# Forgetting attention with plain fp32 values and turned probabilities, the value product of a head pair in two column groups, and sums of squares added up before one reduction

## The chip, the core and the metric

The kernel runs on one core of a Trainium2 chip. The metric is the device time of one execution in microseconds, median of the runs shown. Five engines work side by side, each through its own queue of instructions in a fixed order: PE (matrix products and transposes through the array; its weight loads are listed apart as PEld), DVE (vector work), ACT (activations, copies with a scale), POOL (vector work in SBUF, and issuing of DMAs) and SP (issuing of DMAs). Data lies in SBUF (128 partitions) and in PSUM, where matrix products come out.

## What is computed

One layer for 1024 tokens of width 1024, in fp32, of three sub-layers with RMS norms and residual adds: token mixing, cross-attention to 256 memory tokens, and a SwiGLU feed-forward part. The change lies in token mixing, whose parts are these:

```python
h = rms_norm(x, mix_pre_g); proj = h @ w_in            # u | q | k | v | f_logit
y_ssm = s5_mixer(u, ...)                               # ends in the GLU below
y_fox = forgetting_attention(q, k, v, f_logit)         # 8 heads of 64
y_mix = concat([rms_norm(y_ssm, ssm_out_g), rms_norm(y_fox, fox_out_g)])
x = x + rms_norm(y_mix @ w_out, mix_post_g)
...
g = gelu(y); out = g * sigmoid(g @ glu_w + glu_b)      # end of s5_mixer
...
s = (q @ k.T) * scale + cum_log_f[i] - cum_log_f[j]    # causal, per head
p = softmax(s); out = p @ v                            # per head
```

Both branches are normalised over their 512 channels, so for each token the sum of squares over all channels of `y_ssm`, and over all heads of `y_fox`, is needed.

## The kernel before, in words

**Precision.** Most products are made of three fp32r matmuls (`mm3`, lines 121 to 124): each operand is split (`split`, lines 112 to 119) into a high part, rounded to fp32r by an ACT copy, and the rest, subtracted by DVE; high x high, high x low and low x high are added up in PSUM. Some products are plain fp32 matmuls without splits, which stand in the trace as two instructions each; among them are the sums over partitions with a column of ones (line 237) and the SSM products at lines 485, 537 and 649 to 650. Line 537 puts its 32 weight columns into one of four column groups of the array (`tile_position`).

**Stages.** The input projections and the SSM scan come first, then an attention stage, in which GLU, the SSM half of the output product and the memory tiles run as fillers, then the attention half of the output product, cross-attention and the feed-forward part. The attention stage is driven by `paced(fox(yf), (gp, 0, RATE))` (lines 903 and 1018): after every step of the attention generator about one step of the fillers is traced (`fillers`, line 979: the last v tiles, GLU, `mem_load`, 16 memory tiles, the rest of the output rows, `build_a(0)`). A scheduler then puts each engine's instructions in an order by their place in the program, by priorities and by when their operands and buffers are expected to be free; on the chip that order is fixed.

**v.** `v_tiles` (line 297) makes v in two column halves c of 256 columns (four heads), eight token tiles each. A tile leaves PSUM by an ACT copy with the row scale, is split into high and low (line 300), the two lying side by side per head, and goes to DRAM tensor `v_d` by POOL's queue (line 325). `load_v` (line 805) brings back a head pair by SP's queue.

**Attention** (`fox`, line 705). The loop at line 818 runs over 8 heads x 8 query tiles t of 128 tokens. `scores` is two steps ahead: matmuls, bias and minimum on DVE, exponent on ACT, scaling by the reciprocal sum on DVE or POOL. `turn` (line 761) transposes the probabilities on PE, up to four blocks of 128 to a PSUM bank, and takes them out by `split` (line 772: ACT copy, then DVE subtraction) into two slabs per head and pair of query tiles. `values` (line 774) runs one step later, for each head after every odd t, over a column block of 256 tokens, qc = t // 2: for each of its 2 qc + 2 key tiles two matmuls (lines 782 and 783), whose weights are v's high and low parts together (128 columns), with the high and then the low probabilities moving. So the two halves of PSUM's partitions hold two sums, which ACT (line 789) and DVE (line 790) add; the result is split with its gain (line 791) into `yf`, and squared by ACT.

**Sums of squares.** For heads 0 and 1, each column block's squares are summed over partitions at once by `token_sums` (line 233: two matmuls with ones, and a small DVE copy or addition). From head 2 on, they are added up in a tile `total`, on POOL from head 4 on (line 803), and summed over partitions once at the end (line 840). In `glu` (line 665), each of 8 blocks of 512 tokens x 128 channels is squared by ACT (line 691) and goes through `token_sums` with four matmuls (line 690).

**Buffers.** Large tiles come from a pool of 16 slabs of 8 KB per partition (line 59). The smaller tags of line 193 have one to three buffers; "d" has one, and holds GLU's squares first, `total` later.

`mem_load` (line 955) multiplies the memory tokens by their row scales, four 256-column tiles in one DVE instruction (line 962), ahead of their splits.

## Time and profile before

| | us |
|---|---|
| median of 3 runs | 1432.68 |
| lowest to highest | 1431.65 to 1433.4 |
| span of the profiled execution | 1428.8 |

The profiled execution is told by its span, the time from its first to its last instruction; the runs' times also hold what lies around it. The largest groups of its instructions by busy time are the matmuls of the feed-forward part:

```profile
L1277 PE MATMUL x<-slab,op 128*128 128x512 f32 x984 | 233.3, 389 | 0.5 <-DVE op L115 0.5
L1277 PE MATMUL g<-slab,op 128*128 128x512 f32 x744 | 178.7, 389 | 0.0
```

A row of this view names the line, the engine, the operation, what it writes and reads, its shape and type and how often it ran; then its busy time in us, the mean duration of one in ns, and the idle time of the engine just before, with what ended it. The duration of a matmul includes its way through the array: the next one starts earlier, so the distance of two starts is what a matmul holds PE for. In a timeline, the columns are the start in us from the span's start, the busy time in us, engine, line, operation and how many instructions are merged; an idle time of the engine follows in brackets with its releaser. In a table of stretches, each engine's busy time is followed by its number of instructions, and PEclk is the granted share of PE's clock. In a list of waits, the numbers are the total in us, how often, and the longest.

### The profile page before, as it was taken

The page shows a single profiled execution, that of the slowest core. Times are in us where ns is not written, and L with a number is a line of the kernel's source. Part 1 is how long each engine was busy: PE and PEld are TensorE (multiplying, and loading weights), DVE is VectorE, ACT ScalarE, POOL GpSimd, SP SyncE. Part 2 cuts the span into 40 slices and gives each one's busy share as a digit, 9 for nine tenths or more (in the row PEclk, how much of TensorE's full clock was granted, in tenths as well). Part 3 has the DMA queues.
Part 4 walks back from the last instruction along what each step waited for, and adds up shares of the span by engine and source line. Part 5 has one row for each costly group of instructions (what it writes and reads, how often), then busy time and mean ns, then how long its engine had stood idle before and what let it go on. Part 6 is the DMA issues. An engine that isn't in the chain of part 4 may idle for free.

```text
span 1428.8 us, 20846 instructions
## 1 busy us (share of the span) xinstructions
PE 1390.7 (97%) x7422; PEld 1187.5 (83%) x7422; DVE 1003.7 (70%) x1818; ACT 708.0 (50%) x1421; POOL 410.9 (29%) x432
## 2 busy tenths in 40 slices
PE   7999999999999898999999999999999999999997
PEld 6889898889989886788888788888888888888886
DVE  7839947877888876645557677887766676565565
ACT  6373347777888754543434533333333334444341
POOL 0001000022243134001111367676666661000021
PEclk9999999999999999999999999999999999999999
DMA  6325654165654658323637455454444446965444
GB/s 204 98 80 148 183 192 132 33 204 178 193 153 120 172 164 276 134 74 109 193 112 236 149 190 173 168 181 154 164 156 162 162 155 227 334 219 192 177 162 162
DMA packets 112824, 238.43 MB, mean 167 GB/s; under 512 B 11848, under 2 KB 48712, under 8 KB 112592
## 3 DMA queue, kind: packets, MB, share of 16 engines
q1 hardware_dynamic: 96576, 182.01, 39.8%
q0 software_dynamic: 16144, 55.09, 10.6%
q8 instruction: 58, 0.95, 0.3%
q14 instruction: 46, 0.38, 0.1%
HBM read 168.90 MB, written 76.81 MB: 172 GB/s over the span
## 4 chain that ended last, share of the span: by engine, by line
PE 58%; DVE 1%; DMA 1%; ACT 0%; issue 0%; DVEq 0%; SPq 0%; ACTq 0%
PE x L1277 17%; PE g L1277 13%; PE x L1535 7%; PE g L1535 7%; PE x L123 2%; PE x L124 2%; PE x L122 2%; PE g L122 2%; PE g L124 2%; PE g L123 2%; PE g L1065 1%; DMA a<-t_d 1%; PE g L1173 1%; DVE slab L115 0%; DVE whl L115 0%; DVE c L1056 0%
## 5 line engine op out<-in xcount | busy, mean ns | idle before, releaser
L1277 PE MATMUL x<-slab,op 128*128 128x512 f32 x984 | 233.3, 389 | 0.5 <-DVE op L115 0.5
L1277 PEld LDWEIGHTS x<-slab,op 128*128 128x128 f32 x984 | 184.6, 188 | 39.3 <-DVE op L115 1.0
L1277 PE MATMUL g<-slab,op 128*128 128x512 f32 x744 | 178.7, 389 | 0.0
L115 DVE TENSOR_TENSOR slab<-slab 128x1024 fp32r<-128x1024 f32 (+2 forms) x92 | 110.2, 1207 | 84.7 <-ACT slab L113 82.8
L1277 PEld LDWEIGHTS g<-slab,op 128*128 128x128 f32 x744 | 139.6, 188 | 29.0
L122 PE MATMUL g<-slab,whl 128*128 128x512 f32 (+1 forms) x416 | 151.7, 365 | 0.6 <-ACT whl L113 0.4
L123 PE MATMUL g<-slab,whl 128*128 128x512 f32 (+1 forms) x416 | 148.4, 357 | 0.0
L124 PE MATMUL g<-slab,whl 128*128 128x512 f32 (+1 forms) x416 | 148.2, 357 | 0.0
L113 ACT ACTIVATE slab<-slab 128x1024 fp32r<-128x1024 f32 (+2 forms) x92 | 94.8, 1037 | 106.4 <-DMA slab<-hs_d 81.5
L1535 PE MATMUL g<-slab 128*128 128x512 f32 x462 | 126.6, 389 | 0.0
L1535 PE MATMUL x<-slab 128*128 128x512 f32 x462 | 126.6, 389 | 0.0
L1535 PEld LDWEIGHTS g<-slab 128*128 128x128 f32 x462 | 86.7, 188 | 18.0
L1535 PEld LDWEIGHTS x<-slab 128*128 128x128 f32 x462 | 86.7, 188 | 18.0
L122 PE MATMUL g<-whl,slab 128*128 128x256 f32 (+2 forms) x288 | 87.5, 309 | 9.6 <-ACT whl L113 7.3
L115 DVE TENSOR_TENSOR op<-slab,op 128x512 fp32r<-128x512 f32 x80 | 83.9, 1059 | 11.6 <-ACT op L113 11.3
L1353 POOL TENSOR_TENSOR wt<-wt 128x256 f32<-128x256 f32 x88 | 84.2, 957 | 19.9 <-DMA wt<-in_w_down 16.3
L113 ACT ACTIVATE op<-slab 128x512 fp32r<-128x512 f32 x80 | 50.0, 627 | 77.7 <-PE x L1277 37.5
L122 PEld LDWEIGHTS g<-slab,whl 128*128 128x128 f32 x416 | 78.6, 189 | 11.8 <-ACT whl L113 0.6
L124 PEld LDWEIGHTS g<-slab,whl 128*128 128x128 f32 x416 | 78.4, 189 | 11.6 <-DVE whl L115 0.2
L115 DVE TENSOR_TENSOR whl<-raw,whl 128x1024 fp32r<-128x1024 f32 (+2 forms) x61 | 72.0, 1184 | 22.3 <-ACT whl L113 21.7
L123 PEld LDWEIGHTS g<-slab,whl 128*128 128x128 f32 x416 | 78.6, 189 | 10.6
L123 PE MATMUL g<-whl,slab 128*128 128x256 f32 (+2 forms) x288 | 86.1, 299 | 0.0
(394 smaller groups left out, 3149.3 us busy)
## 6 DMA issues: line engine op xcount, KB each, us to landing
hs_d<-ev POOLq DMA_DIRECT2D x77, 256.0 KB, 2.6
slab<-hs_d SPq DMA_DIRECT2D x35, 512.0 KB
wt<-in_w_down SPq DMA_DIRECT2D x44, 256.0 KB
wt_d<-wt POOLq DMA_DIRECT2D x22, 512.0 KB, 4.8
slab<-in_w_gate SPq DMA_DIRECT2D x20, 512.0 KB
slab<-in_w_up SPq DMA_DIRECT2D x20, 512.0 KB
slab<-wt_d SPq DMA_DIRECT2D x20, 512.0 KB
wd_d<-in_w_down SPq DMA_DIRECT2D x33, 256.0 KB
```

Source lines behind the costliest of these rows:

```text
L113: first = act.activation(out=hi, in_=src, func=AF.Copy, scale=1.0 if mul is None else mul)
L115: (lo_eng or dve).tensor_tensor(out=lo, in0=src, in1=hi.bitcast(F32), op=ALU.subtract)
L122: pe.matmul(ps, lh, rh, start=first, stop=False)
L123: pe.matmul(ps, lh, rl, start=False, stop=False)
L124: pe.matmul(ps, ll, rh, start=False, stop=last)
L1065: pe.transpose(tp[:, k], src[:, (k0 + k) * P:(k0 + k + 1) * P], ident)
L1173: turned = pe.transpose(tp[:, k], h3[:, (4 * n + k) * P:(4 * n + k + 1) * P], ident)
L1277: pe.matmul(ps, x[:, k], y[:, k], start=first and k + n == 0, stop=k == 3 and n == 2, skip_group_check=not first)
L1353: pool.tensor_tensor(out=o, in0=x, in1=y, op=ALU.subtract)
L1535: pe.matmul(banks[n][j], xo[:, u, js], wo[:, v], start=ends[0] and k == 0, stop=ends[1] and k == 2, skip_group_check=onto is not None)
```

## The change

- v stays in fp32: `v_tiles` writes the scaled copy as it is, `v_d` and its loads have half the size, and a load holds two head pairs (`load_v(0)` and `load_v(1)`).
- `turn` takes the turned probabilities out in fp32 by one copy, by DVE and ACT in turn. Three slabs hold a head's (column blocks 0 and 2 share one), until the odd head of the pair is done.
- `values` runs per head pair, after the odd head: for each key tile one fp32 matmul per head, with 64 weight columns each, head 0 in array columns 0 to 63 and head 1 in 64 to 127. The two heads' results then stand in the 128 partitions of one PSUM tile, and go straight from there into the split and the square.
- Squares of all head pairs are added up in `total`, and GLU's rows in `acc`; each is summed over partitions once.
- `mem_load` multiplies tile by tile.

```diff
--- before.py
+++ after.py
@@ -176,7 +176,7 @@
         return rb
 
     qk_d = dram.tile([8, P, S], F32, name="qk_d")
-    v_d = dram.tile([NT, P, 2 * 512], F32, name="v_d")
+    v_d = dram.tile([NT, P, 512], F32, name="v_d")
     h_d = dram.tile([16, NG, HP + P], F32, name="h_d")
     T_d = dram.tile([2, P, 16 * P], F32, name="T_d")
     nc_d = dram.tile([NH, S], F32, name="nc_d")
@@ -230,15 +230,12 @@
         rsqrt_mean(r, ps, D)
         return r, row_bcast(r, L)
 
-    def token_sums(sv, sq, first, p0=0, p1=P):
+    def token_sums(sv, sq):
         n = sv.shape[1]
         ps = g_ps([P, n])
         for j in range(n):
-            pe.matmul(ps[:, j:j + 1], sq[:, j * P:(j + 1) * P], ones[p0:p1, 0:1], start=True, stop=True)
-        if first:
-            dve.tensor_copy(sv, ps)
-        else:
-            dve.tensor_tensor(out=sv, in0=ps, in1=sv, op=ALU.add)
+            pe.matmul(ps[:, j:j + 1], sq[:, j * P:(j + 1) * P], ones[:, 0:1], start=True, stop=True)
+        dve.tensor_copy(sv, ps)
 
     def proj_tile(w, xH, xL, evac, ahead=False):
         halves = []
@@ -295,9 +292,6 @@
         stA.dma_start(out=qk_d[i], in_=o)
 
     def v_tiles(c, xH, xL, r):
-        def evac(ps, r, j, vf, vo):
-            act.activation(out=vf, in_=ps, func=AF.Copy, scale=r[:, j:j + 1])
-            split(vo[:, :, 0], vo[:, :, 1], vf.rearrange("p (h d) -> p h d", d=64))
         if c == 0:
             ws = load_vf()
             ftok = tt("yt", [P, NT, NH])
@@ -312,17 +306,11 @@
                 wh, wl = ws[k // 4]
                 mm3(ps, xH[k][:, ts], xL[k][:, ts], wh[:, k % 4], wl[:, k % 4], k == 0, k == KT - 1)
             vf = t2t([P, 256])
-            if c == 0:
-                vo = t2t([P, 4, 2, 64], F32R)
-            else:
-                if j % 2 == 0:
-                    pair = tt("a", [P, 2, 4, 2, 64], F32R)
-                vo = pair[:, j % 2]
             with tc.high_priority(offset=boost):
-                evac(ps[:, 0:256], r, j, vf, vo)
+                act.activation(out=vf, in_=ps[:, 0:256], func=AF.Copy, scale=r[:, j:j + 1])
                 if c == 0:
                     act.activation(out=ftok[:, j], in_=ps[:, 256:n], func=AF.Copy, scale=r[:, j:j + 1])
-            stA.dma_start(out=v_d.rearrange("t (c j) d -> j (t c) d", j=L)[j, :, c * 512:c * 512 + 512], in_=vo.rearrange("p h t d -> p (h t d)").bitcast(F32))
+            stA.dma_start(out=v_d.rearrange("t (c j) d -> j (t c) d", j=L)[j, :, c * 256:c * 256 + 256], in_=vf)
             yield
 
     def load_vf():
@@ -671,7 +659,7 @@
             split(hl[:, 0], hl[:, 1], w)
             gw.append(hl)
         sv = const.tile([P, NT], F32, name="sv_s")
-        sq, sums = tt("d"), []
+        acc = tt("d")
         for ct in range(4):
             cs = slice(ct * P, (ct + 1) * P)
             hl = slab([P, 2, S])
@@ -686,14 +674,15 @@
                 dve.tensor_tensor(out=y, in0=gl[ct][:, 0, hs].bitcast(F32), in1=gl[ct][:, 1, hs].bitcast(F32), op=ALU.add)
                 dve.scalar_tensor_tensor(out=y, in0=th, scalar=1.0, in1=y, op0=ALU.add, op1=ALU.mult)
                 split(hl[:, 0, hs], hl[:, 1, hs], y, g_out[:, ct:ct + 1])
-                while sums:
-                    token_sums(*sums.pop())
-                act.activation(out=sq[:, hs], in_=y, func=AF.Square)
-                sums.append((sv[:, 4 * h:4 * h + 4], sq[:, hs], ct == 0))
+                if ct == 0:
+                    act.activation(out=acc[:, hs], in_=y, func=AF.Square)
+                else:
+                    act.activation(out=th, in_=y, func=AF.Square)
+                    dve.tensor_tensor(out=acc[:, hs], in0=acc[:, hs], in1=th, op=ALU.add)
                 if h == 1:
                     ys.append(hl)
                 yield
-        token_sums(*sums.pop())
+        token_sums(sv, acc)
         ys_stat.append(sv)
 
     def glu_stats():
@@ -759,62 +748,60 @@
             units[h, t] = sc
 
         def turn(h, t):
-            tt = t % 2
-            if tt == 0:
-                pts[h, t // 2] = slab([P, 8, 256]), slab([P, 8, 256])
-            pth, ptl = pts[h, t // 2]
+            odd = t % 2
+            if t in (0, 2, 6):
+                p = slab([P, 8, 256], F32)
+                if t == 0:
+                    pts[h, 0], pts[h, 2] = p[:, 0:2], p[:, 2:8]
+                else:
+                    pts[h, t // 2] = p
+            pt = pts[h, t // 2]
             sc = units.pop((h, t))
             for k0 in range(0, t + 1, 4):
                 n = min(4, t + 1 - k0)
                 tp = g_ps([P, 4, P])
                 for k in range(n):
                     pe.transpose(tp[:, k], sc[:, (k0 + k) * P:(k0 + k + 1) * P], ident)
-                split(pth[:, k0:k0 + n, tt * P:(tt + 1) * P], ptl[:, k0:k0 + n, tt * P:(tt + 1) * P], tp[:, :n])
-
-        def values(h, qc):
-            r0 = (h % 2) * 64
-            pth, ptl = pts[h, qc]
+                o = pt[:, k0:k0 + n, odd * P:(odd + 1) * P]
+                if (t + k0 // 4) % 2:
+                    dve.tensor_copy(o, tp[:, :n])
+                else:
+                    act.activation(out=o, in_=tp[:, :n], func=AF.Copy)
+
+        def values(hp, qc):
             yp = g_ps([P, 256])
             nk = 2 * qc + 2
             for k in range(nk):
-                w = vs[h // 2][:, k, h % 2]
                 c0 = P if k == nk - 1 else 0
-                pe.matmul(yp[:, c0:], w, pth[:, k, c0:], start=k == 0, stop=False)
-                pe.matmul(yp[:, c0:], w, ptl[:, k, c0:], start=False, stop=k == nk - 1)
-            ft, qs_ = h // 2, slice(qc * 256, qc * 256 + 256)
-            if h % 2 == 0 and qc == 0:
+                for hh in range(2):
+                    w = vs[hp // 2][:, k, (hp % 2) * P + hh * 64:(hp % 2) * P + hh * 64 + 64]
+                    pe.matmul(yp[hh * 64:hh * 64 + 64, c0:], w, pts[2 * hp + hh, qc][:, k, c0:],
+                              start=k == 0, stop=k == nk - 1, tile_position=(0, 64 * hh))
+            qs_ = slice(qc * 256, qc * 256 + 256)
+            if qc == 0:
                 yf.append(slab([P, 2, S]))
-            w = tt("yt", [P, 256])
-            y, sq = w[r0:r0 + 64], w[64 - r0:P - r0]
-            act.activation(out=w[0:64], in_=yp[64:P], func=AF.Copy)
-            dve.tensor_tensor(out=y, in0=yp[0:64], in1=w[0:64], op=ALU.add)
-            split(yf[ft][r0:r0 + 64, 0, qs_], yf[ft][r0:r0 + 64, 1, qs_], y, g_out[r0:r0 + 64, 4 + ft:5 + ft])
-            if h < HA:
-                act.activation(out=sq, in_=y, func=AF.Square)
-                later.append((sv[:, 2 * qc:2 * qc + 2], sq, h == 0, 64 - r0, P - r0))
-                return
-            if h == HA and qc == 0:
-                sums.append(tt("d"))
-            total = sums[0][64 - r0:P - r0, qs_]
-            if h < HA + 2:
-                act.activation(out=total, in_=y, func=AF.Square)
+                if hp == 0:
+                    totals.append(tt("d"))
+            total, = totals
+            split(yf[hp][:, 0, qs_], yf[hp][:, 1, qs_], yp, g_out[:, 4 + hp:5 + hp])
+            if hp == 0:
+                act.activation(out=total[:, qs_], in_=yp, func=AF.Square)
             else:
-                act.activation(out=sq, in_=y, func=AF.Square)
-                pool.tensor_tensor(out=total, in0=total, in1=sq, op=ALU.add)
-
-        def load_v(hp):
-            v = slab([P, NT, 2, P])
-            sp.dma_start(out=v.rearrange("p j h d -> p j (h d)").bitcast(F32),
-                         in_=v_d[:, :, hp * 256:hp * 256 + 256].rearrange("j p c -> p j c"))
-            vs[hp] = v
+                sq = tt("yt", [P, 256])
+                act.activation(out=sq, in_=yp, func=AF.Square)
+                pool.tensor_tensor(out=total[:, qs_], in0=total[:, qs_], in1=sq, op=ALU.add)
+
+        def load_v(c):
+            v = slab([P, NT, 256], F32)
+            sp.dma_start(out=v, in_=v_d[:, :, c * 256:c * 256 + 256].rearrange("j p c -> p j c"))
+            vs[c] = v
 
         seq = [(h, t) for h in range(NH) for t in range(NT)]
-        HA, sums = 2, []
+        totals = []
         lag = 2
         vs = {}
         drain(prepare(0))
         load_v(0)
-        later = []
         for n in range(-lag, len(seq) + 1):
             if n + lag < len(seq):
                 h, t = seq[n + lag]
@@ -823,21 +810,17 @@
                     nxt = prepare(h + 1)
                 if t % 2 and h + 1 < NH:
                     step(nxt)
-                if t == 5 and h % 2 and h + 1 < NH:
-                    load_v(h // 2 + 1)
+                if (h, t) == (3, 5):
+                    load_v(1)
             if 0 <= n < len(seq):
                 h, t = seq[n]
                 turn(h, t)
             yield
             if 0 < n:
                 h, t = seq[n - 1]
-                if t % 2:
-                    values(h, t // 2)
-                    if len(later) > 1 or h >= HA and later:
-                        token_sums(*later.pop(0))
-        while later:
-            token_sums(*later.pop(0))
-        token_sums(sv, sums[0], False)
+                if t % 2 and h % 2:
+                    values(h // 2, t // 2)
+        token_sums(sv, totals[0])
         rsqrt_mean(r_f, sv, 512)
 
     def out_ssm(ys):
@@ -959,8 +942,8 @@
         for k in range(0, KT, 4):
             m = raw([P, 4, 256])
             sp.dma_start(out=m, in_=a["memT"].rearrange("(k p) m -> p k m", p=P)[:, k:k + 4])
-            dve.tensor_tensor(out=m, in0=m, in1=bc(rb, 1, 4), op=ALU.mult)
             for kk in range(4):
+                dve.tensor_tensor(out=m[:, kk], in0=m[:, kk], in1=rb, op=ALU.mult)
                 split(mh[:, k + kk], ml[:, k + kk], m[:, kk], g_mem[:, k + kk:k + kk + 1])
                 if kk % 2:
                     yield
```

## The prediction

> **What bounds the kernel now.** I read the page first (busy shares), then the busy time by stretch of the attention stage, then the waits of PE in that stage.
>
> ```profile
> span 1428.8 us, 20846 instructions
> ...
> PE 1390.7 (97%) x7422; PEld 1187.5 (83%) x7422; DVE 1003.7 (70%) x1818; ACT 708.0 (50%) x1421; POOL 410.9 (29%) x432
> ```
> ```profile
> core 0: us, PE busy (x) PEld busy (x) DVE busy (x) ACT busy (x) POOL busy (x), PEclk, DMA share, GB/s
> 225.00:300.00 75.00, 70.46 (x461) 61.95 (x460) 66.06 (x159) 60.55 (x127) 7.08 (x6) 0.98 0.35 109
> 300.00:460.00 160.00, 157.32 (x1262) 148.96 (x1262) 125.48 (x277) 129.92 (x288) 53.40 (x45) 1.00 0.53 162
> 460.00:513.00 53.00, 46.75 (x310) 42.21 (x308) 40.30 (x78) 37.02 (x76) 7.87 (x9) 0.94 0.58 167
> 282.00:287.00 5.00, 5.00 (x28) 4.50 (x28) 5.00 (x16) 3.95 (x10) 0.00 (x0) 0.66 0.64 188
> ```
> ```profile
> PE g L122 <- DVE slab L117: 2.3, 1, 2.3
> PE g L782 <- ACT slab L113: 2.0, 1, 2.0
> PE g L782 <- DVE slab L115: 1.8, 1, 1.8
> PE g L122 <- DVE sv_f L239: 1.8, 1, 1.8
> ...
> PE g L771 <- DVE yt L790: 1.0, 1, 1.0
> ```
>
> The span is 1428.8 us, and the median of the timed runs, 1432.68, lies 3.9 above it, for what happens before the first and after the last instruction. I make the sum in the span and add the 3.9. PE is busy for 97% of the span. The edits lie almost wholly in the attention stage, 225 to 513 us, where the attention loop and its fillers (GLU, memory tiles, output products) share PE. There PE is busy for 274.5 of 288 us (the three rows added), so it is idle for 13.5. DVE and ACT stand at 66.06 and 60.55 of 75 in the first part, close enough to full that PE waits for them. So PE is the bound in this stage: time taken off PE is worth its full length, time taken off DVE or ACT only what PE now waits for them. The waits also cost clock: after the 1.8 us wait for sv_f (L239), the row 282:287 shows a granted clock of 0.66, and 5 x 0.34 = 1.7 us are lost. The row 460:513 has 0.94 of 53 us, 3.2 lost. Waits and clock come to 13.5 + 75 x 0.02 + 3.2 = 18.2 us.
>
> **Token sums (PE).** Each `token_sums` matmul (L237) is fp32 and stands as two instructions.
>
> ```profile
> 238.31 1.00 PE L237 MATMUL g<-ones,d 128*128 128x1 f32 x8
> 239.17 0.42 PE L771 MATMUL g<-ident,c 128*128 128x128 f32 x2
> ```
> ```profile
> L237 PE MATMUL g<-ones,d 128*128 128x1 f32 x80 | 9.9, 243 | 0.0
> L237 PE MATMUL g<-ones,yt 64*128 64x1 f32 x32 | 4.8, 251 | 0.2 <-DVE slab L115 0.2
> ```
>
> Eight of them hold PE from 238.31 to 239.17, so 0.1075 each (the 243 ns are latency, which overlaps). GLU falls from 64 of the 80 to 16, attention loses the 32 on yt and keeps its 16. Removed: 80 x 0.1075 = **8.6 us** of PE. In exchange DVE adds six rows of 512 (new line in `glu`).
>
> **Value products (PE).** Before, each of 32 calls (8 heads, 4 column blocks) issues two fp32r matmuls per k-step with 128-wide weights.
>
> ```profile
> 276.94 0.28 PE L124 MATMUL g<-whl,slab 128*128 128x256 f32 x1
> 277.06 0.28 PE L782 MATMUL g<-slab 128*128 128x256 f32 x1
> 277.18 0.28 PE L783 MATMUL g<-slab 128*128 128x256 f32 x1
> ...
> 278.80 0.28 PE L783 MATMUL g<-slab 128*128 128x128 f32 x1
> 279.01 0.60 PE L237 MATMUL g<-ones,yt 64*128 64x1 f32 x4
> ```
> ```profile
> L782 PE MATMUL g<-slab 128*128 128x256 f32 x128 | 33.4, 292 | 5.4 <-ACT slab L113 2.0 <-DVE slab L115 1.8 <-ACT t L853 1.7
> L782 PE MATMUL g<-slab 128*128 128x128 f32 x32 | 7.2, 226 | 0.0
> ```
>
> Starts of 256 columns are 0.12 apart, and the last pair of a call, at 128 columns, holds about 0.2 with its exit. L783 has the same counts, so 256 x 0.12 + 64 x 0.09 = 36.5 us. Afterwards each of 16 calls issues, per k-step, one plain fp32 matmul for either head, 64 weight columns each, in two column groups. Again they are 320 instructions, because fp32 counts double. What one costs is shown by the kernel's other plain fp32 matmuls: L485 without column groups, L537 with four.
>
> ```profile
> 91.70 3.82 PE L485 MATMUL g<-slab 128*128 128x128 f32 x32
> 95.28 0.47 PE L122 MATMUL g<-slab,whl 128*128 128x512 f32 x1
> ```
> ```profile
> 124.99 0.28 PE L124 MATMUL g<-whl,slab 128*128 128x264 f32 x1
> 125.10 0.28 PE L122 MATMUL g<-whl,slab 128*128 128x264 f32 x1
> 125.32 1.12 PE L537 MATMUL s<-slab,e 128*32 128x128 f32 x32
> 126.36 0.39 PE L123 MATMUL g<-whl,slab 128*128 128x264 f32 x1
> ```
>
> L485: 3.58 us for 32, 0.112 for 128 columns, so 0.224 for 256. L537: 1.04 us for 32, 0.033 each; four groups do run side by side. Its entry is 0.22 after the matmul before it, where 0.11 to 0.12 is usual; its exit is late by about as much, so a switch of mode costs 0.1. With two groups fully side by side: 256 x 0.224 / 2 + 64 x 0.112 / 2 = 32.3. The first instruction pair of a call starts one group alone and the last ends alone: I add one 256-column instruction per call, 16 x 0.224 = 3.6 (or nothing, if they interleave as finely as L537 does). Switches: 32 x 0.1 = 3.2. In sum 39.1, so values get dearer by **2.6 us**; between -1.0 (no stagger) and, with no overlap at all, 256 x 0.224 + 64 x 0.112 + 3.2 = 67.7, which is +31.2. I take the low side since L537 is the same form with narrower weights.
>
> **Evictions (DVE and ACT).**
>
> ```profile
> L115 DVE TENSOR_TENSOR slab<-g,slab 128x512 fp32r<-128x512 f32 x49 | 33.1, 684 | 1.1 <-ACT slab L113 0.6
> L113 ACT ACTIVATE slab<-g 128x512 fp32r<-128x512 f32 x48 | 28.0, 595 | 5.9 <-PE g L771 5.3
> L117 DVE SCALAR_TENSOR_TENSOR slab<-yt,gains,slab 64x256 fp32r<-64x256 f32 x32 | 20.8, 649 | 1.4 <-ACT slab L113 0.9
> L790 DVE TENSOR_TENSOR yt<-g,yt 64x256 f32<-64x256 f32 x32 | 13.2, 414 | 8.2 <-ACT yt L789 7.8
> L117 DVE SCALAR_TENSOR_TENSOR slab<-g,gains,slab 128x256 fp32r<-128x256 f32 x16 | 7.4, 473 | 0.6 <-ACT slab L113 0.5
> L686 DVE TENSOR_TENSOR t<-slab 128x512 f32<-128x512 f32 x8 | 5.4, 678 | 0.0
> ```
>
> In `turn`, each ACT copy followed by a DVE subtraction becomes one copy, alternately on ACT or DVE. Of the full blocks alone that takes about half of 33.1 from DVE and half of 28.0 from ACT. In `values`, DVE goes from 20.8 + 13.2 = 34.0 to 16 x 0.473 = 7.6, and ACT loses as many operations. GLU adds 6 x 0.678 = 4.1 on DVE. DVE is relieved by some 16.5 + 26.4 - 4.1 = 39 us, a sixth of its 232 in the stage. None of it is PE time; it is worth what PE waits for. Two of the waits shown lose their very cause, L239 (1.8) and L790 (1.0); a third, L782 waiting for L115's subtraction (1.8), loses one of two serial operations. With them go the 1.7 of clock after the first and, by the same size, 1.7 after the last: 1.8 + 1.0 + 1.8 + 3.4 = **8.0 us**. Bounds: none of it (another operation is late instead), or all 18.2. I leave the L117 and L113 waits in place: they name output products and w_out loads, which stay.
>
> For the clock, the Trainium skill, TensorE: Matmul & The Clock Gate, Part 1, says that the clock falls after an idle window of about 3.4 us. The row 282:287 disagrees here, for the wait before it was 1.8 us; by the page the shorter waits would cost no clock, and the sum would gain 3.4 us less, ending at 1422.
>
> **At nothing.** `v_tiles` loses its split; the matmuls at 124.99 and 125.10, quoted above, are those of the v tiles (256 + 8 columns), and they start without a gap, so this relief is hidden by the projection's own matmuls. POOL's queue issues the same 16 v stores at half the size, and SP two v loads instead of four: fewer bytes in stretches where DMA is busy for 0.35 to 0.58. `mem_load` cuts one multiply of 1024 into four of 256: some tenths more on DVE and an earlier first split, covered by PE's other fillers; if uncovered, under 1 us either way. One wait is added: the attention's sum of squares now takes the only "d" buffer at the first odd head, when GLU's sums must be done with it.
>
> ```profile
> 274.52 1.00 PE L237 MATMUL g<-ones,d 128*128 128x1 f32 x8
> 288.52 0.36 PE L782 MATMUL g<-slab 128*128 128x256 f32 x1
> ```
>
> GLU's last sums run at 274.52, and the values of head 1 start at 288.52, so 13 us lie between; were the wait to bite, the Square on ACT would hold the turned copies queued behind it, and PE would run into its full PSUM buffers a few us later.
>
> **Sum.** -8.6 + 2.6 - 8.0 = -14.0: a span of 1414.8, and with 3.9 a time of **1418.7 us**.
>
> **The rivals.** *The column groups run one after another.* Place: the 16 value calls. Then values cost +31.2, and -8.6 + 31.2 - 8.0 = +14.6 gives 1447: slower. It decides once more than half of the possible overlap is missing (values above 53 us instead of 39 to 68). L537's 0.033 per instruction against 0.112 speaks clearly against it. The Trainium skill, TensorE: Matmul & The Clock Gate, Part 3, "The mechanism", would lead here: weight loads overlap running matmuls only where the row groups differ, and both heads use all rows. L537's groups share all rows too, so this trace does not bear that out.
>
> *The slab buffers run out.* There are 16. At head 3, t = 5, I count ys 4, the memory operands 2, yf 2, key slabs 2, v 2 and now 5 of turned probabilities (of three per head, kept until the odd head is done): 17. Before, at most 4 of these were held. Each head pair can then wait once, in `turn`'s evictions or at SP's v load, with the loads queued behind it. Price by the rows: 2.3 of wait and 1.7 of clock, 4 us a pair. Four waits take 16: 1435, slower by 0.15%, and more with the evictions' gain lost, 1443. It decides from three waits on with that loss. For it: the count. Against: values free six slabs soon after, and none of PE's waits above names a load that came late for want of a slab.
>
> *DVE and ACT stay late all the same*: only PE's own sum counts, -6.0, 1427. *All waits go*: -8.6 - 1.0 - 18.2 = -27.8, 1405.
>
> **Chances.** A measurement of this kernel can tell about 0.2% (2.9 us) from no change. Forecast 0.55 (1412 to 1424), late engines 0.17 (to 1428), all waits gone 0.08, slabs 0.12 (1430 to 1443), groups in series 0.08. The range 1404 to 1433 holds the first three and part of the fourth, and leaves out some 0.15. Faster 0.80, within 0.2% 0.07 (mild slab waits, or late engines with worse values), slower 0.13.
>
> **What would show it.** Right: 32 instructions of L237's kind where there were 112; value matmuls of 256 columns on 64 weight columns whose starts average 0.11 to 0.13 us; no subtraction behind `turn`; DVE in 225:513 nearer to 190 than to 232; the clock at 1.00 around 282. Wrong: value starts 0.22 apart on average; new PE or SP waits in `turn` or at the v load; PE idle in the stage still 13 us or more.

## The result, and the profile after

The changed kernel takes 1423.78 us (median of 4 runs, 1421.04 to 1425.92). The kernel before, with a fourth run, takes 1432.16 us (1431.46 to 1433.4). The ratio is 0.9942, with an interval of 0.9928 to 0.9955: faster by 0.58%, 8.4 us, where 14.0 were forecast. Every run whose span is on record lies 1.7 to 1.9 us above it. So the 3.9 us that the prediction added are some 1.8 of this kind, and 2.1 by which the profiled execution of before was quicker than the median.

The page of the changed kernel begins so:

```profile
span 1422.9 us, 20364 instructions
...
PE 1380.0 (97%) x7342; PEld 1165.1 (82%) x7342; DVE 956.9 (67%) x1703; ACT 653.7 (46%) x1293; POOL 406.0 (29%) x428
```

PE has 80 instructions and 10.7 us of busy time less than before, but the span is only 5.9 us shorter. The busy time by stretch, after (the columns are those of the rows of before: window and its length, then busy time of each engine, granted PE clock, DMA):

```profile
187.00:225.00 38.00, 33.82 (x277) 33.43 (x276) 5.49 (x7) 13.49 (x22) 3.24 (x6) 0.96 0.41 128
225.00:300.00 75.00, 67.15 (x416) 58.31 (x415) 64.15 (x145) 54.72 (x112) 7.70 (x7) 0.93 0.35 110
300.00:460.00 160.00, 158.25 (x1291) 141.56 (x1290) 98.18 (x221) 104.24 (x227) 49.76 (x44) 1.00 0.51 154
460.00:513.00 53.00, 47.82 (x325) 39.01 (x325) 34.59 (x69) 30.13 (x70) 9.09 (x8) 0.97 0.67 183
...
199.00:205.00 6.00, 4.37 (x21) 4.17 (x22) 0.69 (x1) 3.61 (x6) 0.55 (x1) 0.72 0.13 43
271.00:280.00 9.00, 7.05 (x38) 7.05 (x39) 7.63 (x16) 7.61 (x16) 1.28 (x1) 0.62 0.18 59
288.00:293.00 5.00, 4.60 (x26) 4.60 (x27) 3.68 (x7) 3.35 (x8) 2.25 (x2) 0.66 0.67 207
```

One stretch ahead of the stage, which the prediction had not looked at, stood like this in the kernel before:

```profile
187.00:225.00 38.00, 36.82 (x313) 36.01 (x312) 13.07 (x21) 19.25 (x36) 3.79 (x7) 1.00 0.55 182
```

DVE's busy time in 225:513 falls from 231.8 to 64.15 + 98.18 + 34.59 = 196.9 us, and ACT's from 227.5 to 189.1. PE profits little. It is idle there for 7.85 + 1.75 + 5.18 = 14.8 us (13.5 before), and in 187:225 for 4.2 (1.2 before). The idle time has gathered in the first part, 225:300, where it rose from 4.5 to 7.85. The waits of PE, after (total, times, longest):

```profile
PE g L237 <- DVE d L681: 5.4, 1, 5.4
PE g L637 <- ACT t L310: 3.8, 1, 3.8
PE g L778 <- ACT slab L769: 2.2, 1, 2.2
PE g L764 <- ACT t L836: 2.0, 1, 2.0
PE g L122 <- ACT t L958: 1.6, 2, 1.3
```

Of the waits that the prediction listed, those on L239, L790, L115 and L117 are gone. The one on L113 has only changed its name: before the last value call ACT's turned copy stands behind a split of w_out that waits for its load, for 2.0 us of PE in before and 2.2 now (L778 for L769), and the prediction had left it in place. Two waits of before stand under new line numbers and are longer: for the copies of SSM output rows (L853, now L836) 2.0 us in one where it was 1.7 in two, and for the v copy (L299, now L310) 3.8 where it was 0.6. The longest is new: PE waits 5.4 us for an addition of GLU's squares (L681, a line that the change brought). The v copy is waited for ahead of the SSM output products (L637). In PE's order of time:

```profile
196.18 0.28 PE L124 MATMUL g<-whl,slab 128*128 128x256 f32 x1
200.27 0.80 PE L637 MATMUL g<-slab 128*128 128x128 f32 x2 [3.82 <-ACT t L310]
...
272.95 1.87 PE L237 MATMUL g<-ones,d 128*128 128x1 f32 x8 [5.37 <-DVE d L681]
...
279.75 0.95 PE L237 MATMUL g<-ones,d 128*128 128x1 f32 x8
...
303.81 0.28 PE L124 MATMUL g<-slab,whl 128*128 128x256 f32 x1
304.01 2.60 PE L778 MATMUL g<-slab 128*64 128x256 f32 x24
306.54 1.09 PE L764 MATMUL g<-ident,c 128*128 128x128 f32 x8
```

GLU's sums run in two halves. PE waits for the first half at 272.95; the second half, the last of GLU's sums, runs at 279.75, where the last sums of before ran at 274.52. What comes last in GLU shows why, first the last addition after the change, then the last square in before:

```profile
276.02 0.68 DVE L681 TENSOR_TENSOR d<-d,t 128x512 f32<-128x512 f32 x1
```
```profile
273.38 0.62 ACT L691 ACTIVATE d<-t 128x512 f32<-128x512 f32 x1
```

So GLU's squares are complete 2.7 us later than before, though PE has less to do. PE is at the first half of the sums sooner, since some of its other work is gone, and then it waits; behind the wait the clock is down (0.62 in 271:280). On ACT's side of the other wait, a copy of head 0's q (L715) stands in front of the v copy and waits for its load:

```profile
199.23 0.63 ACT L715 ACTIVATE a<-d 128x512 fp32r<-128x512 f32 x1 [8.91 <-DMA d<-qk_d]
199.76 0.46 ACT L310 ACTIVATE t<-g,r_x 128x256 f32<-128x256 f32 x1
```

The groups that the change made or reshaped (total busy us, mean ns, idle time before them):

```profile
L778 PE MATMUL g<-slab 128*64 128x256 f32 x256 | 33.1, 396 | 2.2 <-ACT slab L769 2.2
L778 PE MATMUL g<-slab 128*64 128x128 f32 x64 | 7.0, 280 | 0.0
L237 PE MATMUL g<-ones,d 128*128 128x1 f32 x32 | 5.0, 272 | 5.4 <-DVE d L681 5.4
L767 DVE COPY slab<-g 128x512 f32<-128x512 f32 x24 | 16.5, 687 | 12.5 <-PE g L764 12.2
L769 ACT ACTIVATE slab<-g 128x512 f32<-128x512 f32 x24 | 14.2, 591 | 3.6 <-PE g L764 3.5
```

There are 32 instructions of L237's kind, and one copy where a copy and a subtraction were. What a value call holds of PE is read from one start to the next: the call of 24 instructions holds 306.54 - 304.01 = 2.53 us, 0.105 per instruction, and its entry is 0.20 after the matmul before it. The single starts come in pairs 7 ns apart, and a pair lasts 0.216 us: both heads run fully side by side. The calls of 8, 16 and 32 instructions hold 0.80, 1.67 and 3.39 us. Four of each length make 33.6, and 16 entries at 0.09 more than usual make 35.0 us. In before, the calls that no wait cuts hold 0.41, 0.90, 1.38 and 1.85 us, and eight of each make 36.3: **-1.3 us** (forecast +2.6).

### The profile page after: what moved, and what is told of

Read it like the earlier page. It is cut to its first block, busy times and chain, and to the rows that moved or that the text cites. A ratio compares the mean times of both kernels' runs of the same rounds, so it can differ in the third digit from the quotient of the medians.

```text
span 1422.9 us, 20364 instructions
## 1 busy us (share of the span) xinstructions
PE 1380.0 (97%) x7342; PEld 1165.1 (82%) x7342; DVE 956.9 (67%) x1703; ACT 653.7 (46%) x1293; POOL 406.0 (29%) x428
## 4 chain that ended last, share of the span: by engine, by line
PE 59%; DVE 1%; ACT 0%; issue 0%; DVEq 0%; ACTq 0%
PE x L1260 17%; PE g L1260 13%; PE x L1518 7%; PE g L1518 7%; PE x L123 2%; PE x L124 2%; PE x L122 2%; PE g L122 2%; PE g L123 2%; PE g L124 2%; PE g L1048 1%; PE g L1156 1%; DVE slab L115 0%; DVE whl L115 0%; DVE c L1039 0%; DVE rst L141 0%
## 5 line engine op out<-in xcount | busy, mean ns | idle before, releaser
L115 DVE TENSOR_TENSOR slab<-slab 128x1024 fp32r<-128x1024 f32 (+2 forms) x92 | 110.5, 1207 | 84.6 <-ACT slab L113 82.6
L113 ACT ACTIVATE slab<-slab 128x1024 fp32r<-128x1024 f32 (+2 forms) x92 | 95.0, 1037 | 105.0 <-DMA slab<-hs_d 75.0
L122 PE MATMUL g<-whl,slab 128*128 128x256 f32 (+2 forms) x288 | 88.5, 313 | 8.3 <-ACT whl L113 7.3
L115 DVE TENSOR_TENSOR whl<-raw,whl 128x1024 fp32r<-128x1024 f32 (+2 forms) x61 | 71.5, 1175 | 30.9 <-ACT whl L113 30.6
L115 DVE TENSOR_TENSOR op<-slab,op 128x512 fp32r<-128x512 f32 x80 | 83.4, 1053 | 11.5 <-ACT op L113 11.3
L124 PE MATMUL g<-whl,slab 128*128 128x256 f32 (+2 forms) x288 | 86.9, 302 | 0.0
L123 PE MATMUL g<-whl,slab 128*128 128x256 f32 (+2 forms) x288 | 86.8, 301 | 0.0
```

The costliest lines, as they stand in the source:

```text
L113: first = act.activation(out=hi, in_=src, func=AF.Copy, scale=1.0 if mul is None else mul)
L115: (lo_eng or dve).tensor_tensor(out=lo, in0=src, in1=hi.bitcast(F32), op=ALU.subtract)
L122: pe.matmul(ps, lh, rh, start=first, stop=False)
L123: pe.matmul(ps, lh, rl, start=False, stop=False)
L124: pe.matmul(ps, ll, rh, start=False, stop=last)
```

## The experiments

The main theory was that the two new waits (5.4 and 3.8 us, and the clock after them) cost what is missing, and that without them the kernel comes near the forecast. The rival was that PE is no longer what sets the end in this stage: a wait that is taken away only brings PE sooner to the next operand that isn't ready. The ratios below are to the kernel before, on the same chip; the changed kernel's is 0.9942.

### The two halves of the change, each alone

*The value part alone*: the changed kernel with GLU's token sums as they were.

```diff
-        acc = tt("d")
+        sq, sums = tt("d"), []
...
-                if ct == 0:
-                    act.activation(out=acc[:, hs], in_=y, func=AF.Square)
-                else:
-                    act.activation(out=th, in_=y, func=AF.Square)
-                    dve.tensor_tensor(out=acc[:, hs], in0=acc[:, hs], in1=th, op=ALU.add)
+                while sums:
+                    token_sums(*sums.pop())
+                act.activation(out=sq[:, hs], in_=y, func=AF.Square)
+                sums.append((sv[:, 4 * h:4 * h + 4], sq[:, hs], ct == 0))
```

> The changed kernel with GLU's sums as before (eight calls of token sums over single blocks), all else changed. If GLU's part as written brings a wait of 5.4 us on its last addition and about 3.4 us of clock, against some 3.5 us of waits and clock that its old form had, and saves 48 instructions x 0.1075 = 5.2 us of PE, then the two cancel: 1423 to 1425, with no wait of 5 us at the sums. If GLU's part is worth what PE saves on it: 1428 to 1430.

Measured: 1423.27 us, ratio 0.994 (0.9922 to 0.9957), not to be told from the whole change. PE waits 0.6 us at GLU's sums. *The GLU part alone*, put into the kernel before by the reverse of that diff:

> The kernel before with GLU's part alone (squares added up in one tile, one call of token sums). If the new wait eats what PE saves: 1430 to 1433, and PE waits for the last addition of squares for 3 us or more. If GLU's part is worth 5.2 us of PE: 1426 to 1428.

Measured: 1430.85 us, ratio 0.999 (0.9977 to 1.0002). Its waits on PE:

```profile
PE g L237 <- DVE d L693: 3.4, 1, 3.4
PE g L122 <- DVE slab L117: 2.3, 1, 2.3
PE g L783 <- ACT slab L113: 2.1, 1, 2.1
```

So the GLU part takes 48 x 0.1075 = 5.2 us off PE and is worth some 1.4 us alone (between 3.3 and nothing) and about none beside the rest (to within some 3 us). The wait at the sums comes with it in either kernel: 3.4 us here, 5.4 there. It also lengthens GLU. From the start of the first square to the last write of the tile of squares GLU takes 38.1 us in before and 42.0 with the GLU part alone; with the value part alone it takes 33.9, and with both 36.1.

The value part took 3.4 (token sums) + 1.3 (values) = 4.7 us off PE and is worth 8.6 (6.2 to 11.2), so something pays on top; its relief of DVE and ACT is the likely source. The profiles bear this out, one of each kernel. I count PE from 187 us to a common point behind the stage, its first transposes ahead of cross-attention (585.4 us in before, 576.8 with the value part, 579.6 with the whole change). Up to there PE is busy for 377.8, 373.9 and 367.2 us and idle for 20.6, 15.9 and 25.4. The value part shortens both; the GLU part on top of it takes 6.7 us of busy time away and brings 9.5 of idle time. In the stretch around GLU's end the two kernels stand so, first the value part alone:

```profile
230.00:273.00 43.00, 42.38 (x261) 36.49 (x259) 35.94 (x85) 28.71 (x58) 1.08 (x2) 1.00 0.26 80
```

and then the whole change:

```profile
230.00:273.00 43.00, 37.55 (x212) 31.18 (x210) 38.61 (x87) 30.83 (x63) 2.86 (x3) 0.99 0.25 80
```

PE is 98.6% busy without the GLU part. With it PE is 87% busy, and DVE, with five of the six additions in this stretch, stands at 38.61 of 43 us.

### Four attempts on the wait for GLU's sums

*A buffer of its own for the square*, so that ACT's next tanh need not wait for the addition (in `yt`, in two halves of 256):

```diff
-                    act.activation(out=th, in_=y, func=AF.Square)
-                    dve.tensor_tensor(out=acc[:, hs], in0=acc[:, hs], in1=th, op=ALU.add)
+                    for q in range(2):
+                        qs = slice(q * 256, q * 256 + 256)
+                        sq = tt("yt", [P, 256])
+                        act.activation(out=sq, in_=y[:, qs], func=AF.Square)
+                        o = acc[:, h * 512 + q * 256:h * 512 + q * 256 + 256]
+                        dve.tensor_tensor(out=o, in0=o, in1=sq, op=ALU.add)
```

> The changed kernel, but GLU's squares go through a small buffer of their own in two halves of 256, so that the tanh's buffer is free as early as before. If the wait of 5.4 us comes from the next block's tanh waiting for that buffer: PE's wait at the token sums falls below 2 us, the clock's fall at 272 us goes, and the time is 1415 to 1419. If DVE's load alone makes GLU late: the wait stays and the time is 1422 to 1425.

Measured: 1424.22 us, ratio 0.9938 (0.9921 to 0.9955). The wait falls to 3.7 us, and the time stays.

```profile
272.90 1.02 PE L237 MATMUL g<-ones,d 128*128 128x1 f32 x4 [3.69 <-DVE d L685]
```

*The addition on POOL* (`pool.tensor_tensor` in place of `dve.tensor_tensor`):

> The changed kernel with GLU's additions of squares on POOL instead of DVE. If the stretch from the first scores to the end of GLU is set by DVE's load (38.6 of 43 us busy in the changed kernel), 4.1 us less on DVE lets GLU end earlier: PE's wait at the token sums falls from 5.4 to 1.5 to 3 us, and the time is 1419 to 1422. If the chain of one GLU block after the other sets it, the longer addition on POOL leaves the wait at 5 us or more: 1423 to 1426.

Measured: 1425.45 us, ratio 0.9962 (0.9947 to 0.9977). PE waits 4.4 us for POOL's addition now, and 1.6 more for a new operand, DVE's row maxima:

```profile
PE g L237 <- POOL d L681: 4.4, 1, 4.4
PE g L637 <- ACT t L310: 3.9, 1, 3.9
...
PE s L733 <- DVE nlr L740: 1.6, 1, 1.6
```

*The scaling of the probabilities of heads 0 and 1 on POOL* at t = 1, 3, 5, so that DVE has more room while GLU runs:

```diff
-            if t in POOL_T and h > 1:
+            if t in POOL_T:
```

> The changed kernel with the scaling of the probabilities of heads 0 and 1, t = 1, 3, 5, on POOL instead of DVE, as heads 2 to 7 have it: some 3 us less on DVE before GLU's end. If DVE's load sets the stretch: PE's wait at the token sums falls to 2 to 4 us, the time is 1420 to 1422. If the chain of GLU's blocks sets it: wait 5 us or more, 1423 to 1425.

Measured: 1423.12 us, ratio 0.9942 (0.9924 to 0.996), and the wait for the sums is 4.1 us. DVE's busy time in 230:273 did not fall (39.23 us), so the room that was meant for the chain was not there. What fills it is DVE's own instructions, which take longer beside POOL's:

```profile
248.10 1.47 POOL L745 TENSOR_TENSOR c<-c,nlr 128x768 f32<-128x768 f32 x1 [8.29 <-PE s L736]
```
```profile
248.11 2.00 DVE L117 SCALAR_TENSOR_TENSOR slab<-t,gains,slab 128x512 fp32r<-128x512 f32 x1
```

L117 takes 0.75 us on this shape otherwise. Three of GLU's DVE instructions that start in this stretch take 3.2 us longer than usual together. With the additions on POOL it is the same (five of GLU's 128x512 instructions take 1.30 to 1.84 us there), so neither shift to POOL is a clean test of how full DVE is.

*No scaling at all*, a kernel that leaves part of the computation out:

```diff
-            if t in POOL_T and h > 1:
-                pool.tensor_tensor(out=sc[:, :ke], in0=sc[:, :ke], in1=rl.broadcast_to([P, ke]), op=ALU.mult)
-            else:
-                dve.tensor_scalar(out=sc[:, :ke], in0=sc[:, :ke], scalar1=rl, scalar2=None, op0=ALU.mult)
```

> The changed kernel without the scaling of the probabilities by the reciprocal sums (the probabilities are used unscaled): 27.7 us less on DVE, 18.7 on POOL, and one operation less between the exponent and the transposes; PE's work is untouched. If PE's waits come from late DVE and ACT: of the 17.6 us of idle time and lost clock in the loop much goes, 1411 to 1417. If PE's queue bounds the stage and the waits are fixed by its order: 1421 to 1425.

Measured: 1420.12 us, ratio 0.993 (0.9914 to 0.9946). By the page DVE loses 29.7 us and POOL 21.5; the time falls by 1.7 by the ratios, 4.0 by the spans. Both waits stay:

```profile
PE g L237 <- DVE d L681: 4.6, 1, 4.6
PE g L637 <- ACT t L310: 4.6, 1, 4.6
```

DVE's busy time in 230:273 is down to 34.56 us here, and the wait hardly shrinks. So the sums don't hang on how full DVE is. What is left is the order of a chain (tanh, products, split, square, addition, half by half); that is argued, no run isolates it.

### The wait for the v copy, and both waits together

*Head 0's q and k copies behind the last v copy traced before them* in the order of the engines:

```diff
+    vcopy = []
...
-                act.activation(out=vf, in_=ps[:, 0:256], func=AF.Copy, scale=r[:, j:j + 1])
+                vcopy.append(act.activation(out=vf, in_=ps[:, 0:256], func=AF.Copy, scale=r[:, j:j + 1]))
...
-            return tc.issue_after(last[-1].ins) if last else ExitStack()
+            return tc.issue_after((last or vcopy)[-1].ins)
```

> The changed kernel, but head 0's q and k copies on ACT are issued behind the v copies traced before them. If ACT's wait for q's load, ahead of a v copy, is what holds PE for 3.8 us at 196 us and costs 1.7 us of clock: that wait goes and the time is 1417 to 1420. If PE only waits later instead: 1422 to 1425.

Measured: 1422.39 us, ratio 0.9926 (0.9912 to 0.9939).

```profile
198.19 0.49 PE L639 MATMUL g<-slab 128*128 128x128 f32 x2 [0.56 <-ACT t L312]
```

The wait is 0.56 us where it was 3.82, which shows that the order on ACT made it. From the first SSM output product to the first scores it is 38.0 us instead of 41.6 (37.3 in before). Of these 3.6 us the time shows some 2.3 by the ratios and 1.4 by the medians, and the two intervals overlap.

*With this, both shifts to POOL*:

> The two moves to POOL together, and head 0's q copies behind the v copies on ACT. If DVE's load sets the stretch and the two waits are independent: the PE wait at the token sums below 2 us, the one at 196 us gone, 1415 to 1419. If waits only move to the next late operation: 1421 to 1424.

Measured: 1424.66 us, ratio 0.9956 (0.9941 to 0.9971). Both named waits are down, to 0.7 and 0.6 us, and others have come, the longest for the first head pair's square (L790), which stands on ACT behind a weight split that waits for its load:

```profile
PE g L766 <- ACT d L790: 4.2, 1, 4.2
PE s L735 <- DVE nlr L742: 3.2, 2, 3.0
PE g L780 <- ACT slab L771: 2.2, 1, 2.2
```

*With it, GLU's token sums two filler steps later*:

```diff
-        token_sums(sv, acc)
-        ys_stat.append(sv)
+        ys_stat.append((sv, acc))
...
-        sv, = ys_stat
+        (sv, acc), = ys_stat
+        token_sums(sv, acc)
...
+        load = mem_load(r_mem[0], mem)
+        for _ in range(2):
+            next(load)
+            yield
         glu_stats()
-        for _ in mem_load(r_mem[0], mem):
-            step(rows)
+        for _ in load:
+            step(rows, 2)
             yield
```

> The changed kernel with head 0's q copies behind the v copies on ACT, and GLU's token sums two filler steps later, behind the first two steps of the memory load. If PE's two named waits can be covered with other matmuls of PE that are ready: both waits below 1 us, 1416 to 1419. If PE only meets the next late operand sooner: 1421 to 1425.

Measured: 1422.32 us, ratio 0.9937 (0.9921 to 0.9953). Again both named waits are short, 0.2 and 0.6 us, and again the time is not shorter:

```profile
PE s L735 <- DVE nlr L742: 3.6, 2, 3.0
PE g L766 <- DVE sv_s L238: 3.1, 1, 3.1
PE g L766 <- POOL c L747: 1.9, 1, 1.9
```

The second of these is GLU again: L238 is the copy of GLU's sums, which stands on DVE behind splits of the memory tokens. PE's idle time in 225:300 stays, 9.3 us in the kernel with the shifts to POOL and 7.9 in this one, where the changed kernel has 7.85:

```profile
225.00:300.00 75.00, 65.70 (x394) 56.28 (x393) 64.44 (x130) 50.57 (x105) 22.00 (x18) 0.91 0.34 102
```
```profile
225.00:300.00 75.00, 67.10 (x406) 57.31 (x405) 64.85 (x143) 52.36 (x107) 7.65 (x6) 0.91 0.34 106
```

With this the main theory falls. Two different orders without the two named waits are worth at most what the v copy alone is worth, since PE waits as long at other places of the same stretch.

### What a microsecond of PE is worth

*The scores without their second matmul*, which leaves the low part of the keys out of the result:

```diff
-                pe.matmul(ps[:, c0:c1], qt, ka[:, 0, c0:c1], start=True, stop=False)
-                pe.matmul(ps[:, c0:c1], qt, ka[:, 1, c0:c1], start=False, stop=not dg)
+                pe.matmul(ps[:, c0:c1], qt, ka[:, 0, c0:c1], start=True, stop=not dg)
```

> The changed kernel without the second matmul of the scores (k's low part is left out of the product; the split that makes it stays). It takes 96 matmuls, 48 x 0.235 + 16 x 0.18 + 16 x 0.123 + 16 x 0.115 = 18.0 us of PE, off the attention loop and nothing off the other engines. If PE's queue bounds the stage all along: 1405 to 1408. If the chains over DVE and ACT now bound much of it, PE only waits longer: 1413 to 1421, with more idle time of PE.

Measured: 1414.93 us, ratio 0.989 (0.9873 to 0.9907).

```profile
225.00:300.00 75.00, 65.01 (x422) 55.63 (x422) 65.61 (x150) 56.75 (x117) 7.84 (x8) 0.95 0.37 112
300.00:460.00 160.00, 151.85 (x1247) 134.85 (x1244) 103.06 (x230) 107.41 (x233) 50.85 (x44) 0.98 0.53 162
```

PE's busy time falls by 1380.0 - 1361.6 = 18.4 us, but the time only by 7.4 (by the ratios) to 11.4 (by the spans). Of the other half, PE's idle time in these two windows takes 8.5 us: 9.99 + 8.15, where it was 7.85 + 1.75.

*One head after the other within a value call*, which adds PE time:

```diff
-            for k in range(nk):
-                c0 = P if k == nk - 1 else 0
-                for hh in range(2):
+            for hh in range(2):
+                for k in range(nk):
+                    c0 = P if k == nk - 1 else 0
```

> The changed kernel with the value matmuls of a call ordered head by head instead of alternating. If PE starts matmuls strictly in the order of its queue, the two column groups then run one after another: starts about 0.21 us apart, some 29 us more in all, 1450 to 1456. If the array takes the other group's matmuls ahead of a waiting one, the pairs of starts 7 ns apart stay: 1422 to 1426.

Measured: 1437.57 us, ratio 1.004 (1.0022 to 1.0058), slower than before, and between the two expected times.

```profile
305.49 0.28 PE L124 MATMUL g<-slab,whl 128*128 128x256 f32 x1
305.70 4.38 PE L778 MATMUL g<-slab 128*64 128x256 f32 x24
310.00 0.77 PE L764 MATMUL g<-ident,c 128*128 128x128 f32 x5
```

The same 24 instructions hold 4.30 us instead of 2.53, and all value calls 54.9 us instead of 35.5 (the 33.6 from above, and 1.9 more in the last call, which a wait cuts in two there). The single starts are 0.216 us apart, except for some eight around the border between the heads. Calls of 8 instructions lose nothing (0.81 us). Of 19.4 us more on PE, 14.0 come through by the ratios.

### The multiply of `mem_load` in one again

```diff
+            dve.tensor_tensor(out=m, in0=m, in1=bc(rb, 1, 4), op=ALU.mult)
             for kk in range(4):
-                dve.tensor_tensor(out=m[:, kk], in0=m[:, kk], in1=rb, op=ALU.mult)
```

> The changed kernel with the memory load's multiply in one instruction of 1024 again. If that edit is worth nothing, as forecast: 1422 to 1425. If the earlier first split helped PE through the wait after GLU: 1425 to 1427.

Measured: 1423.15 us, ratio 0.9951 (0.9934 to 0.9967): no difference from the changed kernel's 0.9942.

No kernel here that computes the whole result is clearly faster than the changed one. The best, 1422.3 and 1422.4 us, overlap with it.

## Why the prediction was right and where it was wrong

**Direction and range** held: faster by 0.58%, inside 1404 to 1433, 5.1 us above the forecast. The rivals by which it would have been slower did not come: the column groups run side by side, and no wait in PE's list names a load that came late for want of a slab. The rival by which DVE and ACT stay late came in part. PE's own sum is -8.6 - 1.3 = -9.9 us where -6.0 stood, so of the 8.0 that stalls were to give nothing came, and 1.5 were lost on top. That the total still lies in the forecast's own band (1412 to 1424) is owed to the values, which came out 3.9 us better than forecast; that part is luck.

**Token sums, -8.6.** The removal is as counted, 112 instructions to 32. Its worth is not. The attention's 32 (3.4 us) belong to the value part, which paid more than its PE time; no run prices them by themselves. GLU's 48 (5.2 us) are the part that alone brings 1.4 us and beside the rest about none. This is the step that failed: "PE is the bound in this stage: time taken off PE is worth its full length". The 97% of the page and the 274.5 busy of 288 us showed that PE was seldom idle, not that its operands would be ready sooner if PE were quicker. The six additions were priced as 4.1 us of DVE's relief and not as links of GLU's chain, which they made 2.2 to 3.9 us longer. GLU's last sums ran at 274.52 before and run at 279.75 after; the operand that they need came later, although PE had less to do. With 18.4 us less on PE the kernel gains 7.4 to 11.4, with 19.4 more it loses 14.0: near this point a microsecond of PE is worth 0.4 to 0.7.

**Values, +2.6.** They came out at -1.3. The stagger of 3.6 us does not exist, since the pairs start 7 ns apart. The switches cost 0.09 on entry, 1.4 in sum, where 3.2 stood.

**Evictions and stalls, -8.0.** The relief itself was sized well: DVE 196.9 us in the stage, where "nearer 190 than 232" was asked. In the value part alone it is worth 8.6 - 4.7 = 3.9 us (1.5 to 6.5), if PE's 4.7 count in full. The prediction's own sum for this part was -3.4 + 2.6 - 8.0 = -8.8 and the run gave -8.6, but by two misses that cancel: values 3.9 us cheaper, stalls worth 4.1 less. That agreement is luck. That the named waits would go was right; that they would go with nothing in their place was not. The clock shows the same: it is at 1.00 around 282 as forecast, but down at 271 to 280. "PE idle in the stage still 13 us or more" was named as the sign of being wrong, and it reads 14.8.

**At nothing.** `mem_load` was right. So was the one "d" buffer: the last of GLU's sums run at 279.75, and the first square of the heads goes into it at 289.91, behind no wait for it. `v_tiles` was wrong by a wait: the v copy that PE needs comes to stand behind a copy of q that waits 8.91 us for its load. That ACT's order is the cause is shown by the kernel that changes this order alone. Why the scheduler chose that order (a buffer of `a` that is free sooner is my guess) was not tried. Its worth is some 2 us, not clear of the spread.

**The sum.** Of the 14.0 us forecast, 8.4 came. The missing 5.6 are, within the intervals, GLU's 5.2. What stays open is which chain sets the pace once PE is quick. The waits name, in different kernels, GLU's additions, DVE's row maxima (L735 for nlr), the turned copies and the v copies. Neither DVE's load (the kernel without scaling), nor the buffer that the tanh and the square share (its own kernel), nor the two longest waits came out as the one cause. The traces fit many short chains with fixed places in PE's queue; no run isolates one.

**The clock.** After the 3.8 us wait the 199.00 to 205.00 stretch has a clock of 0.72, and after the 2.0 us wait for L836 the 288.00 to 293.00 stretch has 0.66. The Trainium skill, TensorE: Matmul & The Clock Gate, Part 1, has the clock fall after an idle window of about 3.4 us. The first case agrees, the second does not, as the 1.8 us wait of before did not.

## What to carry to other kernels

A busy share of 97% does not make an engine the bound: before pricing time taken off it at full length, look up for each place where it consumes another engine's result how long ago that result was ready. Where it was just ready, the saving ahead of that place turns into a wait. An operation added to such a place's chain on another engine makes the wait longer. A removed wait is worth something only up to the next operand that is late, so list the second and third in line and sum only the difference. Where two column groups share the array, issue them in turn, not one after the other.

## What the runs showed of the hardware that was not expected

- Plain fp32 matmuls of 64 weight columns in two column groups, issued in turn, start in pairs 7 ns apart, and a pair of 256 columns takes 0.216 us. The Trainium skill, TensorE: Matmul & The Clock Gate, Part 3, "The mechanism", has a sentence by which weight loads overlap running matmuls only where the row groups differ. These two groups use the same rows, and 24 such instructions, each with its weight load, hold 2.53 us, so the trace disagrees with that sentence.
- Issued one group after the other, the same 24 hold 4.30 us. Only about four instructions on either side of the border run side by side, by the spacing of the starts (5 to 210 ns there, mostly 216 elsewhere); calls with four instructions per head lose nothing.
- DVE instructions stretch beside POOL's: a split's subtraction on 128x512 (L117) took 2.00 us beside a POOL multiply of 1.47, where 0.75 is usual. Work moved from DVE to POOL can therefore come back on DVE as time.
- Executions of one kernel spread by more than their difference from a neighbour: the kernel before ran between 1427.41 and 1436.57 us in 17 runs, so that a term of 2 us can't be read from two profiles, and hardly from the ratios of a few runs.
